# Two weight sums of each group of seven made by accumulating transfers, and the first feed-forward's first product without such a group

## The chip, the core and the metric

The kernel runs on one core of a Trainium2 chip. The metric is the device time of the whole program in microseconds (us); lower is better. The engines that matter here are TensorE (PE in the profile, with PEld for its weight loads), VectorE (DVE), ScalarE (ACT), GpSimd (POOL) and SyncE (SP), which issues nearly all DMAs.

## What is computed

The reference is a trunk of two layers on 256 rows of width 1024. Each layer is a feed-forward, a token mixer (a convolution module in layer 0, latent attention in layer 1), and a second feed-forward; a last norm follows. So there are four feed-forwards:

```python
D_MODEL, SEQ, DEPTH, D_FF = 1024, 256, 2, 2816

def swiglu_ffn(h, w1, w3, w2):
    return (jax.nn.silu(h @ w1) * (h @ w3)) @ w2

for i in range(DEPTH):
    h = h + 0.5 * swiglu_ffn(rmsnorm(h, ffn_norm1[i]), ffn1_w1[i], ffn1_w3[i], ffn1_w2[i])
    m = rmsnorm(h, mix_norm[i])
    h = h + (conv_module(m, ...) if i % 2 == 0 else mla(m, positions, ...))
    h = h + 0.5 * swiglu_ffn(rmsnorm(h, ffn_norm2[i]), ffn2_w1[i], ffn2_w3[i], ffn2_w2[i])
return rmsnorm(h, final_norm)
```

All numbers are float32.

## The kernel before

**Products.** Every float32 operand is split into a high part (`hi`, type fp32r) and a low part (`lo`, what is left), and a product is made of three matmuls (`mm3`, L330: L332 high row by low weight, L335 high by high, L336 low row by high weight). One such matmul has a 128x128 stationary block of rows and a moving weight of 128x512. The 256 rows are two blocks of 128 (`tb`).

**Weights.** They stream in blocks of 1 MB (128 x 2048 floats, eight KB to a partition), in the order of the list `blocks` (L122 to L148). `load` (L218) fetches a block through SP's queue into one of four `raw` buffers (`RAW_BUFS`), ScalarE casts its two halves to `hi` (L246), and VectorE subtracts `lo = raw - hi` (L247). There are five pairs of `hi` and `lo` (`W_BUFS`), so at most four blocks are cast ahead of the one in use. A pair comes free when TensorE is done with its block; a raw buffer when its last reader is done.

**Feed-forwards.** In each, the up product (w1 and w3) goes in six chunks of columns (loop at L876), the last one half as wide; a chunk is four blocks of weights, each used by 24 matmuls. SiLU, the product of both halves and a turn through memory (`turn`, L838, with `turn_blocks`, L465) make the gates `Gh` and `Gl`, the rows of the down product (w2), which is the class `Rows` (L745).

**Groups of seven.** One chunk of the up product (the fourth, `c == 3`, by `SEVEN_UP`) and the first four blocks of the down product (`SEVEN_DOWN`) are made, in each of the four feed-forwards, as a two by two block product with seven block products instead of eight. The two row blocks by two halves of the inner dimension are on one side, four weight blocks (W11, W12, W21, W22) on the other. `seven_products` (L366) makes the seven, each of 12 matmuls on one combination of weights and one of rows; combinations of its results are copied and added between them (L383, L386, L388, L395). The combinations of rows are made once by `whole_rows` (L347; L349), `sums_of_rows` (L338; L344) and `forms_of` (L352; L361 and L362 split them).

The combinations of weights are made by `load_seven` (L189), called for j = 0 to 6 in the place of seven blocks. It fetches the four blocks by `fetched` (L182, its DMA is L184) at j = 0 (two), 1 and 2, and sums in place, with whole-tile subtractions on VectorE by its helper `sub` (L200): at j = 1 `b11 = W12 - W11` and `b12 = W12 - W22`; at j = 2 `b11 = W22 - b11`; at j = 6 `b11 = W21 - b11`. The product j uses `b11, b11, b11, b21, b12, b22, b11`, each cast by ScalarE in halves (L214) and subtracted by VectorE (`sub` again, so also L200).

**Order.** A planner puts the instructions of each engine in order when the program is built; what is marked `urgent` (L252) goes ahead. Each engine then runs its own list in that order, and an instruction that waits holds up what stands behind it. `order` (L154) adds an order by hand; `behind` (L158) keeps a cast behind the last urgent instructions of its engine. GpSimd has little to do outside the convolution: the norms' small scalars (L429 to L432).

Of the kernel before, what the change touches and what calls it, by code (L numbers as in the profile page):

```python
# [16 lines left out]
ALU = mybir.AluOpType  # L17
# [28 lines left out]

SEVEN_UP = {0: (3,), 1: (3,), 2: (3,), 3: (3,)}
SEVEN_DOWN = (0, 1, 2, 3)  # L50

CONV_DVE = (0, 2, 4)
# [37 lines left out]
def trunk(ctx: ExitStack, tc: tile.TileContext, x, xt, first, pos, invf, gfin, wdw,  # L90
          f1w13, f1w2, f2w13, f2w2, cw1, cw2, wa, wuq, wukv, wo, wpair, out):
    nc = tc.nc
# [12 lines left out]
    def uid(s):  # L105
        n_uid[0] += 1
        return f"{s}_{n_uid[0]}"
# [16 lines left out]
    for i in range(2):  # L124
        for w13, w2 in ((f1w13, f1w2), (f2w13, f2w2)):

            n_ffn = 2 * i + (w13 is f2w13)
            for cc_ in range(5):
                if cc_ in SEVEN_UP.get(n_ffn, ()):
                    four = [w13[i, m, 2 * cc_ + a_] for a_ in range(2) for m in range(2)]  # L130
# [23 lines left out]
    def order(ins, first):  # L154
        tc.add_manual_dep(ins.ins, first.name, mybir.DependencyInfo(
            mybir.DependencyClass.NoSync, mybir.DependencyReason.DATA), reason="order")

    def behind(ins):  # L158

        for first in ahead_of.get(ins.ins.engine, [])[-BEHIND:]:  # L160
            order(ins, first)
# [20 lines left out]
    def fetched(src):  # L182
        raw = rawp.tile([P, HB], F32, tag="raw", name=uid("raw"))
        dma = nc.sync.dma_start(raw, src)  # L184
        if turns:
            order(dma, turns[-1].ins)
        return raw

    def load_seven(j, four, b, pieces):  # L189
        hi = wp.tile([P, HB], F32R, tag="hi", name=uid("hi"))  # L190
        lo = wp.tile([P, HB], F32R, tag="lo", name=uid("lo"))
        n = len(loaded)
        if j == 0:
            b[11], b[12] = fetched(four[0]), fetched(four[1])
        elif j == 1:
            b[22] = fetched(four[3])
        elif j == 2:
            b[21] = fetched(four[2])
        def sub(out, left, right):
            ins = nc.vector.tensor_sub(out, left, right)  # L200
            behind(ins)
            return ins

        if j == 1:
            sub(b[11], b[12], b[11])
            sub(b[12], b[22], b[12])
        elif j == 2:
            sub(b[11], b[22], b[11])
        elif j == 6:
            sub(b[11], b[21], b[11])  # L210
        raw = b[(11, 11, 11, 21, 12, 22, 11)[j]]
        for i in range(pieces):
            c = slice(i * HB // pieces, (i + 1) * HB // pieces)
            casts[n, i] = nc.scalar.copy(hi[:, c], raw[:, c]), sub(lo[:, c], raw[:, c], hi[:, c].bitcast(F32))  # L214
            behind(casts[n, i][0])
        return hi, lo

    def load(src, pieces=1):  # L218
        if isinstance(src, tuple) and src[0] == "seven":
            return load_seven(*src[1:], pieces)  # L220
# [31 lines left out]
    def urgent(f):  # L252

        def g(*args, **kw):
            traced = nc.cur_bb.bb.instructions
            n = len(traced)
            with tc.high_priority():
                r = f(*args, **kw)
            last = {ins.engine: ins for ins in traced[n:]}
            for engine, ins in last.items():  # L260
                ahead_of.setdefault(engine, []).append(ins)
            return r
        return g

    def load_ahead(ahead=W_BUFS - 2):
        load_to(min(len(blocks), n_used[0] + ahead))
# [5 lines left out]
    def weights(n=1, more=True):  # L272
        out = []
        for _ in range(n):
            n_used[0] += 1
            if more:
                load_ahead()
            else:
                load_ahead(0)
            out.append(loaded[n_used[0] - 1])  # L280
        return out
# [48 lines left out]
    def mm3(o, ah, al, bh, bl, start, stop, after=(), seeded=False):  # L330

        mm = nc.tensor.matmul(o, ah, bl, start=start, stop=False, skip_group_check=seeded)  # L332
        for a in after:
            order(mm, a.ins)
        nc.tensor.matmul(o, ah, bh, start=False, stop=False, skip_group_check=seeded)  # L335
        return nc.tensor.matmul(o, al, bh, start=False, stop=stop, skip_group_check=seeded)  # L336

    def sums_of_rows(x11, x12, x21, x22):  # L338


        sums = [(0, x22, x21, x22, ALU.add), (2, x21, x11, x21, ALU.subtract), (1, x11, x22, x11, ALU.subtract),
                (3, x12, x12, x11, ALU.subtract)]
        for n, out, left, right, op in sums:
            nc.vector.tensor_tensor(out, left, right, op=op)  # L344
        return sorted(((n, out) for n, out, *_ in sums), key=lambda s: s[0])
# [20 lines left out]
    def seven_products(xh, xl, forms, banks):  # L366


        def rows(a, tb):
            k = slice(4 * a, 4 * a + 4)  # L370
            return xh[:, k, tbs(tb)], xl[:, k, tbs(tb)]

        def product(a, b, fresh):
            load_ahead(W_BUFS - 1)
            (hi, lo), = weights(1, False)
            for k in range(4):
                c = slice(k * 512, k * 512 + 512)
                mm3(b, a[0][:, k], a[1][:, k], hi[:, c], lo[:, c], fresh and k == 0, k == 3, (), True)

        n0 = n_used[0]  # L380
        c11, c21, c12, c22 = banks[0, 0], banks[1, 0], banks[0, 1], banks[1, 1]
        product(rows(0, 0), c11, True)
        urgent(nc.scalar.copy)(c21, c11)  # L383
        product(forms[0], c22, True)
        kept = tmp.tile([P, 512], F32, tag="s", name=uid("p5"))
        last = urgent(nc.scalar.copy)(kept, c22)  # L386
        product(forms[1], c21, False)
        add = urgent(nc.vector.tensor_add)(c12, c21, kept)  # L388
        order(casts[n0 + 5, 0][1], add.ins)
        for high, low in gates[-NT:]:  # L390
            order(high, last.ins)
            order(low, add.ins)
        product(rows(1, 0), c11, False)
        product(forms[2], c21, False)
        add = urgent(nc.vector.tensor_add)(c22, c21, kept)  # L395
        order(casts[n0 + 6, 0][1], add.ins)
        product(forms[3], c12, False)
        product(rows(1, 1), c21, False)
# [8 lines left out]
    def tbs(tb):  # L407
        return slice(tb * P, (tb + 1) * P)
# [336 lines left out]
    class Rows:  # L745
# [6 lines left out]
        def seven(self, forms):  # L752
            seven_products(self.zh, self.zl, forms, self.o)
# [74 lines left out]
    def ffn(X, make_next, beside=lambda: None, apart=False):  # L828
        n = n_ffns[0]
        n_ffns[0] += 1  # L830
        with tc.tile_pool(name=uid("ffn"), bufs=1) as act:
            return ffn_in(act, X, make_next, beside, apart, SEVEN_UP.get(n, ()), n in SEVEN_DOWN)

    def ffn_in(act, X, make_next, beside, apart, seven_up, seven_down):
# [41 lines left out]
        for c in range(6):  # L876
# [7 lines left out]
            if seven_up and c == min(seven_up) - (1 if X.whole else 2):  # L884
                forms = forms_of(sums_of_rows(*whole_rows(X.xh, X.xl)), Gh[:, 14:], Gl[:, 14:])
            if c in seven_up:
                for key in ((0, 0), (0, 1), (1, 1), (1, 0)):
                    u[key] = bank("A", "u")
                seven_products(X.xh, X.xl, forms, {(tb, m): b for (m, tb), b in u.items()})
                beside()  # L890
                beside()
            if both and seven_down:
                z11, z21, z12, z22 = (rows4[:, n, :] for n in range(4))
                down_sums = sums_of_rows(z11, z12, z21, z22)
                first_form = forms_of(down_sums[:1], *(act.tile([P, 2, S], F32R, tag=tag, name=uid(tag))
                                                       for tag in ("s1h", "s1l")))
# [910 lines left out]
```

## Time and profile before

| what | value |
|---|---|
| median of three runs | 907.87 us (907.69 to 908.38) |
| the profiled execution, its own time | 905.75 us |
| its span, first to last instruction | 903.8 us |
| mean granted TensorE clock | 0.995 |
| matmuls | 4209 |
| DMA | 198.94 MB, 220 GB/s on the mean |

The profile is of one execution. A line of a group names the source line, the engine, the operation, what is written from what, and a count; then busy us and mean ns of one, and after the second bar the idle time of the engine before them with what ended it. A matmul overlaps the next one, so its own length says less than the number of matmuls in a stretch. "PEclk" is the clock that TensorE was granted, 1.00 being full speed. A view of stretches gives, for each, its length, then the busy time and the count of instructions of each engine, the granted clock, the busy share of the 16 DMA engines and their GB/s. A view in order of time gives start and length in us, engine, line, operation and count, and in brackets the idle time before and what ended it. A DMA line gives the count, the KB of one and the median us from issue to landing.

### The profile page before, as it was taken

The numbers are of one execution on the slowest core, as the hardware profiler recorded it, in microseconds if no ns is written. First come the engines' busy times: TensorE is split into PE (matmuls) and PEld (weight loads), VectorE is DVE, ScalarE is ACT, GpSimd is POOL, SyncE is SP. The second block draws the span as 40 slices with busy tenths as digits, with TensorE's granted clock in tenths as the row PEclk, the third lists the DMA queues.
The fourth block names the chain that finished last, engine by engine and source line by source line (L and its number), as shares of the span: only waits on it lengthen the run. The fifth ranks groups of instructions, "written<-read, shape, count | busy, mean of one in ns | idle before, by whom it ended". The sixth has DMA issues, their size and how long they took to land.

```text
span 903.8 us, 12258 instructions
## 1 busy us (share of the span) xinstructions
PE 890.2 (98%) x4209; PEld 744.1 (82%) x4209; DVE 765.3 (85%) x1104; ACT 580.7 (64%) x1005; POOL 104.2 (12%) x227
## 2 busy tenths in 40 slices
PE   9998999999999999999999999999999999999997
PEld 7886787898998888887878888888899888888886
DVE  6899999669998988999588999994768588999963
ACT  7965849579886745766475466573767576465752
POOL 1000000049972000000010000000500010000000
PEclk9999999999999999999999999999999999999999
DMA  9883947825415873948849459396544449378551
GB/s 337 324 278 96 341 171 264 356 86 202 141 47 158 317 270 99 368 150 330 303 133 342 161 171 381 89 397 216 190 175 169 158 137 350 101 257 319 173 200 47
DMA packets 71054, 198.94 MB, mean 220 GB/s; under 512 B 12368, under 2 KB 41936, under 8 KB 51664
## 3 DMA queue, kind: packets, MB, share of 16 engines
q1 hardware_dynamic: 70560, 197.47, 61.5%
q8 instruction: 33, 0.54, 0.2%
q10 hardware_dynamic: 432, 0.69, 0.2%
q14 instruction: 29, 0.24, 0.1%
HBM read 181.87 MB, written 16.25 MB: 219 GB/s over the span
## 4 chain that ended last, share of the span: by engine, by line
PE 76%; DVE 11%; DMA 6%; issue 2%; ACT 2%; SPq 1%; DVEq 0%; ACTq 0%
PE u L332 11%; PE u L336 11%; PE u L335 11%; PE o L332 8%; PE o L335 8%; PE o L336 8%; DVE lo L200 3%; PE u L993 3%; PE gate L993 3%; DMA raw<-in_f2w 3%; DVE raw L200 2%; PE u L403 2%; PE o L1229 2%; DVE lo L247 1%; DMA hd<-rows 1%
## 5 line engine op out<-in xcount | busy, mean ns | idle before, releaser
L247 DVE TENSOR_TENSOR lo<-raw,hi 128x1024 fp32r<-128x1024 f32 (+1 forms) x228 | 266.8, 1211 | 35.0 <-ACT hi L246 33.7
L246 ACT CAST hi<-raw 128x1024 fp32r<-128x1024 f32 (+1 forms) x230 | 228.6, 1044 | 78.7 <-DMA raw<-in_f2w 30.5
L332 PE MATMUL u<-lo,Xh 128*128 128x512 f32 x592 | 231.7, 391 | 2.6 <-DVE lo L200 1.9
L335 PE MATMUL u<-hi,Xh 128*128 128x512 f32 x592 | 231.0, 390 | 0.0
L336 PE MATMUL u<-hi,Xl 128*128 128x512 f32 x592 | 230.8, 391 | 0.0
L214 ACT CAST hi<-raw 128x1024 fp32r<-128x1024 f32 x112 | 111.4, 1049 | 65.5 <-DVE raw L200 55.6
L200 DVE TENSOR_TENSOR lo<-raw,hi 128x1024 fp32r<-128x1024 f32 x112 | 132.4, 1215 | 6.6 <-ACT hi L214 6.6
L332 PEld LDWEIGHTS u<-lo,Xh 128*128 128x128 f32 x592 | 111.6, 188 | 27.9 <-DVE lo L200 3.9
L336 PEld LDWEIGHTS u<-hi,Xl 128*128 128x128 f32 x592 | 111.5, 188 | 24.3 <-DVE Xl L457 0.5
L335 PEld LDWEIGHTS u<-hi,Xh 128*128 128x128 f32 x592 | 111.5, 188 | 23.0
L336 PE MATMUL o<-hi,Gl 128*128 128x512 f32 (+1 forms) x276 | 106.6, 386 | 0.0
L335 PE MATMUL o<-hi,Gh 128*128 128x512 f32 (+1 forms) x276 | 106.5, 386 | 0.0
L332 PE MATMUL o<-lo,Gh 128*128 128x512 f32 (+1 forms) x276 | 106.2, 387 | 0.2 <-DVE lo L200 0.2
L429 POOL TENSOR_TENSOR ms<-ss 128x1 f32<-128x1 f32 x16 | 8.1, 512 | 607.2 <-ACT junk L421 607.2
L200 DVE TENSOR_TENSOR raw<-raw,raw 128x2048 f32<-128x2048 f32 x32 | 73.0, 2280 | 2.4 <-DMA raw<-in_f1w 1.1
L332 PEld LDWEIGHTS o<-lo,Gh 128*128 128x128 f32 x276 | 51.8, 188 | 11.5 <-DVE lo L200 1.0
L336 PEld LDWEIGHTS o<-hi,Gl 128*128 128x128 f32 x276 | 51.8, 188 | 10.6
L335 PEld LDWEIGHTS o<-hi,Gh 128*128 128x128 f32 x276 | 51.9, 188 | 10.2
L1082 DVE SCALAR_TENSOR_TENSOR acc<-V,dw,acc 128x128 f32<-128x128 f32 (+1 forms) x174 | 53.9, 391 | 0.0
L1103 ACT ACTIVATE prod<-V,dw 128x128 f32<-128x128 f32 (+1 forms) x128 | 45.8, 415 | 2.0 <-POOL Y L1104 1.0
L845 ACT CAST Gh<-gb 128x512 fp32r<-128x512 f32 (+1 forms) x32 | 18.0, 565 | 32.2 <-DMA gb<-gd 32.2
L789 DVE SCALAR_TENSOR_TENSOR h<-o,rh,h 128x512 f32<-128x512 f32 (+1 forms) x18 | 12.9, 719 | 29.5 <-PE o L336 29.5
(265 smaller groups left out, 1311.9 us busy)
## 6 DMA issues: line engine op xcount, KB each, us to landing
raw<-in_f2w SPq DMA_DIRECT2D x66, 1024.0 KB, 6.5
raw<-in_f1w SPq DMA_DIRECT2D x62, 1024.0 KB, 6.9
raw<-in_cw SPq DMA_DIRECT2D x12, 1024.0 KB, 5.6
gd<-gt SPq DMA_DIRECT2D x160, 64.0 KB, 3.1
gb<-gd SPq DMA_DIRECT2D x24, 256.0 KB, 2.8
rows<-gd SPq DMA_DIRECT2D x16, 256.0 KB, 3.0
raw<-in_wo SPq DMA_DIRECT2D x4, 1024.0 KB, 4.7
hd<-rows SPq DMA_DIRECT2D x56, 64.0 KB, 2.2
```

What stands on the lines that cost most here:

```text
L200: ins = nc.vector.tensor_sub(out, left, right)
L214: casts[n, i] = nc.scalar.copy(hi[:, c], raw[:, c]), sub(lo[:, c], raw[:, c], hi[:, c].bitcast(F32))
L246: casts[len(loaded), i] = (nc.scalar.copy(hi[:, c], raw[:, c]), low.tensor_sub(lo[:, c], raw[:, c], hi[:, c].bitcast(F32)))
L247: low.tensor_sub(lo[:, c], raw[:, c], hi[:, c].bitcast(F32)))
L332: mm = nc.tensor.matmul(o, ah, bl, start=start, stop=False, skip_group_check=seeded)
L335: nc.tensor.matmul(o, ah, bh, start=False, stop=False, skip_group_check=seeded)
L336: return nc.tensor.matmul(o, al, bh, start=False, stop=stop, skip_group_check=seeded)
L403: mm = nc.tensor.matmul(o, al if kind == "x" else ah, bl if kind == "l" else bh, start=start and n == 0, stop=stop and n == len(kinds) - 1)
L993: mm = nc.tensor.matmul(u[:, t], w[:, c], X.x[:, k, t], start=(k == 0), stop=(k == KT - 1))
L1082: dve_last.append(nc.vector.scalar_tensor_tensor(out if j == j1 - 1 else y, v, w, y, op0=ALU.mult, op1=ALU.add))
L1103: prods_last.append(nc.scalar.activation(p, v, AF.Copy, scale=w))
L1229: p = nc.tensor.matmul(o[tb, d], (Zl if kind == "x" else Zh)[:, f, tbs(tb)], (lo if kind == "l" else hi)[:, c], start=(f, kind) == (0, "l" ...
```

## The change

The first feed-forward (number 0) leaves `SEVEN_UP`: its fourth chunk is made like the others, with four blocks of 24 matmuls. The other seven groups stay. In them, the two sums at j = 1 are no longer made by VectorE: GpSimd issues two DMAs that read a weight block a second time and add it, on the way, to the tile in SBUF (`accum_op`). Such a transfer adds only, so the signs are turned: `b11 = W11 + W12`, `b12 = W12 + W22`; the sums at j = 2 and 6 stay on VectorE as additions, and the sums of rows and two of the additions after products change their signs to match. The new DMAs have no order by hand.

```diff
-SEVEN_UP = {0: (3,), 1: (3,), 2: (3,), 3: (3,)}
+SEVEN_UP = {1: (3,), 2: (3,), 3: (3,)}
...
-        def sub(out, left, right):
-            ins = nc.vector.tensor_sub(out, left, right)
+
+        def sub(out, left, right, op=ALU.subtract):
+            ins = nc.vector.tensor_tensor(out, left, right, op=op)
             behind(ins)
             return ins
 
         if j == 1:
-            sub(b[11], b[12], b[11])
-            sub(b[12], b[22], b[12])
+
+            nc.gpsimd.dma_start(b[11], four[1], accum_op=ALU.add)
+            nc.gpsimd.dma_start(b[12], four[3], accum_op=ALU.add)
         elif j == 2:
-            sub(b[11], b[22], b[11])
+            sub(b[11], b[22], b[11], ALU.add)
         elif j == 6:
-            sub(b[11], b[21], b[11])
+            sub(b[11], b[21], b[11], ALU.add)
...
-        sums = [(0, x22, x21, x22, ALU.add), (2, x21, x11, x21, ALU.subtract), (1, x11, x22, x11, ALU.subtract),
-                (3, x12, x12, x11, ALU.subtract)]
+        sums = [(0, x22, x21, x22, ALU.subtract), (2, x21, x11, x21, ALU.subtract), (1, x11, x22, x11, ALU.subtract),
+                (3, x12, x12, x11, ALU.add)]
...
-        add = urgent(nc.vector.tensor_add)(c12, c21, kept)
+        add = urgent(nc.vector.tensor_sub)(c12, kept, c21)
...
-        add = urgent(nc.vector.tensor_add)(c22, c21, kept)
+        add = urgent(nc.vector.tensor_sub)(c22, kept, c21)
```

## The prediction

> **What bounds the kernel now.** I read the page first: the share of each engine, and the chain that ended last.
>
> ```profile
> PE 890.2 (98%) x4209; PEld 744.1 (82%) x4209; DVE 765.3 (85%) x1104; ACT 580.7 (64%) x1005; POOL 104.2 (12%) x227
> PE 76%; DVE 11%; DMA 6%; issue 2%; ACT 2%; SPq 1%; DVEq 0%; ACTq 0%
> ```
>
> TensorE is busy nearly the whole span, and the chain runs through it. So a change is worth what it does to the number of matmuls, and to the few places where they do not follow each other at full pace. A busy PE is modelled, so I count matmuls per stretch instead: the views of stretches, first around the group that the change drops (first feed-forward, fourth chunk), then inside it.
>
> ```profile
> 60.00:100.00 40.00, 34.81 (x137) 27.23 (x136) 38.63 (x39) 24.20 (x35) 0.00 (x0) 0.91 0.58 198
> 100.00:140.00 40.00, 40.00 (x178) 33.05 (x177) 37.47 (x40) 24.67 (x39) 0.00 (x0) 1.00 0.61 214
> 76.00:84.00 8.00, 5.12 (x17) 3.80 (x16) 7.03 (x9) 7.51 (x9) 0.00 (x0) 0.79 0.37 100
> 90.00:100.00 10.00, 8.05 (x28) 5.85 (x27) 10.00 (x13) 9.38 (x16) 0.00 (x0) 0.83 0.88 326
> PE u L332 <- DVE lo L200: 4.8, 2, 2.9
> ```
>
> The columns are the stretch, its length, busy us (count) of PE, PEld, DVE, ACT and POOL, the granted clock, the DMA share and GB/s. A clean 40 us holds 178 matmuls, so one takes 40 / 178 = 0.2247 us. The 40 us of this group hold 137: 41 x 0.2247 = **9.2 us are lost there**. The last row, from the waits of that same stretch, says for what: the low part of a weight (L200, a DVE subtraction in the group's loader). The wait itself is 4.8 us; the rest is the slow pace after it, with a granted clock of 0.79 and 0.83 in the two stretches with the waits. DVE is busy 38.6 of these 40 us, so it is DVE that is late.
>
> The seven groups that stay lose far less. In a clean 20 us there are 89 to 90 matmuls:
>
> ```profile
> 140.00:160.00 20.00, 19.83 (x87) 15.88 (x86) 18.61 (x19) 17.95 (x35) 0.00 (x0) 1.00 0.90 326
> 360.00:380.00 20.00, 19.90 (x88) 16.16 (x87) 20.00 (x21) 15.62 (x17) 0.00 (x0) 1.00 0.96 352
> 400.00:420.00 20.00, 19.73 (x87) 15.80 (x86) 20.00 (x23) 15.04 (x21) 0.00 (x0) 1.00 0.61 218
> 520.00:540.00 20.00, 19.90 (x88) 16.20 (x87) 17.74 (x20) 11.90 (x15) 0.00 (x0) 1.00 0.47 152
> 800.00:820.00 20.00, 19.90 (x89) 16.14 (x88) 20.00 (x21) 14.95 (x17) 0.00 (x0) 1.00 0.95 350
> 840.00:860.00 20.00, 20.00 (x89) 16.23 (x88) 20.00 (x23) 15.93 (x22) 0.00 (x0) 1.00 0.59 209
> ```
>
> Against 90 they lack 3 + 2 + 3 + 2 + 1 + 1 = 12 matmuls, 12 x 0.2247 = 2.7 us in all. That is the most that freeing DVE in them can give.
>
> **Part one: the first feed-forward's group goes.** A group is seven products of 12 matmuls, 84; the plain chunk is two halves by two row blocks by eight by three, 96. So 12 x 0.2247 = +2.7 us. DVE loses, by these rows, four sums, six low parts (three weights of two pieces), one whole-row sum, four sums of rows, four low parts of forms:
>
> ```profile
> L200 DVE TENSOR_TENSOR lo<-raw,hi 128x1024 fp32r<-128x1024 f32 x112 | 132.4, 1215 | 6.6 <-ACT hi L214 6.6
> L200 DVE TENSOR_TENSOR raw<-raw,raw 128x2048 f32<-128x2048 f32 x32 | 73.0, 2280 | 2.4 <-DMA raw<-in_f1w 1.1 <-DMA raw<-in_f2w 1.0
> L344 DVE TENSOR_TENSOR xs<-xs 128x512 f32<-128x512 f32 x16 | 10.9, 682 | 0.0
> L362 DVE TENSOR_TENSOR Gl<-xs,Gh 128x512 fp32r<-128x512 f32 x16 | 10.8, 684 | 0.0
> L349 DVE TENSOR_TENSOR xs<-Xh,Xl 128x2048 f32<-128x2048 f32 x4 | 9.1, 2285 | 0.0
> ```
>
> 4 x 2.28 + 6 x 1.215 + 2.285 + 4 x 0.682 + 4 x 0.684 = 9.1 + 7.3 + 2.3 + 2.7 + 2.7 = 24.1 us less on an engine that was behind by 9. What is late next? The four weights are still fetched, now by the plain loader, with 24 matmuls (5.4 us) to each instead of 12, and the DMA runs at 198 GB/s in that stretch, while one MB in 5.4 us asks for about 195; after it 0.99 of the DMAs was a catching up that is now spread. The two products of SiLU that were urgent are so no longer; 24 us of free DVE hide that. I take all of the 9.2 us back: **-9.2 + 2.7 = -6.5 us**. Bounds: nothing back, +2.7; all back, -6.5.
>
> **Part two: in seven groups two DVE sums become two accumulating transfers.** Per group DVE loses 2 x 2.28 = 4.6 us. SP's queue is not touched; POOL gets the two issues. Both signs of a sum have one price (L344 holds both). No row shows an accumulating transfer, so the question is by when it must have landed. Take the down group of the second feed-forward, from the order of time (start, length):
>
> ```profile
> 381.21 2.36 DVE L200 TENSOR_TENSOR lo<-raw,hi 128x1024 fp32r<-128x1024 f32 x2 [0.78 <-ACT hi L214]
> 384.56 2.29 DVE L200 TENSOR_TENSOR raw<-raw,raw 128x2048 f32<-128x2048 f32 x1 [0.99 <-DMA raw<-in_f2w]
> 386.97 2.00 ACT L214 CAST hi<-raw 128x1024 fp32r<-128x1024 f32 x2 [1.24 <-DVE raw L200]
> 401.56 0.39 PE L332 MATMUL o<-lo,s1h 128*128 128x512 f32 x1
> 404.28 0.40 PE L332 MATMUL o<-lo,rows 128*128 128x512 f32 x1
> ```
>
> The first row is the first product's low parts: they end at 383.57, and only then may the first matrix be added to in place. The second row is the sum that goes. The fourth is the second product's first matmul, which needs that sum cast; the fifth the third product's, which needs a further sum on top. After the landing: cast 1.05 and low part 1.2, ready 2.3 us later, so the second product allows 401.56 - 383.57 - 2.3 = 15.7 us. For the third, both pieces must be cast and their low parts taken (2.00 + 1.2, about 3.4 with the handovers), then the sum 2.28 and a cast and low part 2.3: 8.0 us, so 404.28 - 383.57 - 8.0 = **12.7 us from the last low part to the landing**. The same for the up group:
>
> ```profile
> 326.56 2.31 DVE L200 TENSOR_TENSOR lo<-raw,hi 128x1024 fp32r<-128x1024 f32 x2
> 349.48 0.39 PE L332 MATMUL u<-lo,Gh 128*128 128x512 f32 x1
> ```
>
> The third product starts 12 x 0.2247 = 2.7 us after the second, at 352.2: 352.2 - 328.87 - 8.0 = **15.3 us**. The second matrix's sum is wanted only for the fifth product, 8 us later still, so it may land second.
>
> The price by the nearest rows: one MB alone, one MB among the group's own fetches (first the down group's, then the up group's), the rate in the latter stretch, and a small POOL instruction:
>
> ```profile
> raw<-in_wo SPq DMA_DIRECT2D x4, 1024.0 KB, 4.7
> raw<-in_f2w SPq DMA_DIRECT2D x4, 1024.0 KB, 8.0
> raw<-in_f2w SPq DMA_DIRECT2D x4, 1024.0 KB, 7.4
> DMA packets 1253, 4.94 MB, mean 411 GB/s; under 512 B 142, under 2 KB 654, under 8 KB 692
> L432 POOL TENSOR_TENSOR R<-ms,neghalf 128x1 f32<-128x1 f32 x12 | 6.8, 565 | 1.0
> ```
>
> It must read a MB of SBUF besides the MB of weights. Low end: like a lone plain one, 4.7. High end: like two crowded ones in a row and an issue on POOL, 2 x 8.0 + 0.6 = 16.6 (down), 2 x 7.4 + 0.6 = 15.4 (up). I take one crowded landing, one more MB at 411 GB/s (2.5 us), and an issue: 8.0 + 2.5 + 0.6 = 11.1 (down), 10.5 (up), because the group's own fetches are still on the way when it starts, and nothing is behind them:
>
> ```profile
> 384.00:391.00 7.00, 7.00 (x33) 5.79 (x32) 6.43 (x6) 3.14 (x4) 0.00 (x0) 1.00 0.76 306
> 391.00:404.00 13.00, 13.00 (x59) 10.78 (x58) 12.97 (x15) 7.71 (x12) 0.00 (x0) 1.00 0.37 95
> ```
>
> That is under 12.7 and 15.3: hidden by the weights that are cast ahead. (The Trainium skill, Collectives: The Full Stack, section on the bandwidth ceiling, says that an adding transfer moves half the bytes of a copy in the same time, because it reads two sources; the bare transport of one MB at 411 GB/s would become 5.1 us by that. No run yet shows it; it would put the landing inside both limits too.)
>
> Queues behind the new waits: POOL is idle in all these rows (0.00), so its two issues hold up nothing until the next norm. ACT's cast of the sum waits for the landing; behind it stand casts of gates and forms, on DVE the low part and behind it the gates' products and turns. They bear the same limit, as long as the planned order puts them ahead of the cast. What it gives: at most the 2.7 us; but these lie at the sixth and seventh products, whose own sum and casts crowd DVE at the end of the group, 15 us after the sums that go. I take **0**, keeping 0 to -2.7.
>
> **The sum.** Against the profiled execution, 905.75 us (span 903.8): 905.75 - 6.5 = 899.25. The median of the runs shown, 907.87, lies 2.12 above it, so **901.4 us**.
>
> **Rivals.**
> *The transfers land too late (slower).* At the high end, 16.6 and 15.4, the third product is late by 3.9 us in each of four down groups and 0.1 in each of three up groups: 15.9 us, 917.3. It decides from 12.7 us on: at 14.3 (four times 1.6) part one is eaten up, and from 14.8 the kernel is slower by over 0.2%. For it: the second transfer shares the DMAs with the first, or may be issued ahead of it. Against: the DMAs at 0.37 from 391 on. Chance 0.26.
> *POOL is slow to issue beside a busy DVE.* DVE runs without a break from 384 to 404 (6.43 of 7, 12.97 of 13). If an issue had to wait for an unbroken run of one DVE group, 4.6 us such as the two sums together, the landing comes to 15.7 and 15.1: 4 x 3.0 = 12 us, 913.4. Chance 0.04. (The Trainium skill, SBUF — State Buffer, section Who interferes with whom, is where this comes from: a transfer issued by GpSimd starves while VectorE holds the shared port pair, though it excepts the two-input operation that fills DVE here. That exception is why the chance is small.)
> *The first feed-forward stays late.* If half of the 9.2 us comes back elsewhere before 140 us, because the plain chunk's weights now arrive no earlier (0.99 DMA share after 100), then 907.87 + 2.7 - 4.6 = 906.0. DVE's 24 us speak against. Chance 0.13. That the dropped group had no real cost would be this case's far end, 910.6.
>
> **How the numbers follow.** Forecast 0.57 (its own range 898 to 904, the 2.7 us either way); the rivals 0.26, 0.04, 0.13. From 898 to 918 holds nearly all of the forecast and of the third rival, and half of the first two: about 0.83. A measurement can tell 0.2%, 1.8 us: faster (below 906.05) is the forecast plus half of the third rival, 0.63; same, the rest of it and the onset of the first, 0.08; slower 0.29.
>
> **What would show it.** Between 60 and 100 us about 178 matmuls, granted clock 1.00, and no wait for L200: part one right. TensorE's 4209 matmuls becoming 4221. The landing of the accumulating transfer in each group below 12.7 us after the first product's low parts: part two right; above it, waits of PE for L200 in every down group at its third product, and the clock below 1.00 there, prove the first rival. An issue on POOL of several us proves the second. DVE's busy time should fall by 24 + 7 x 4.6 = 56 us, to about 709; if the time falls no more than part one says, DVE was no bound in the seven groups.

## The result, and the profile after

The changed kernel takes **954.69 us** (median, 952.96 to 960.98), the kernel before in the same comparison 907.78 (905.99 to 908.38): a ratio of **1.053, 95% interval 1.048 to 1.058**. It is slower, 53 us above the forecast and outside the range. The profiled execution took 954.62 us, its span is 952.8, the mean granted clock 0.983. Of the runs below, one of experiment 5, the profiled one (945.1 us), counts as slow: that experiment's ratio is of its other three (924.57 to 930.79 us), and what is read in its trace is of that run.

First the page of the kernel after: the engines, the chain that ended last, the queue of GpSimd's own DMAs (packets, MB, share of 16 engines over the span), the gates' casts on ScalarE, and the issues of eight of the fourteen accumulating transfers.

```profile
PE 904.2 (95%) x4221; PEld 752.4 (79%) x4221; DVE 711.4 (75%) x1069; ACT 571.6 (60%) x993; POOL 118.0 (12%) x241
q0 software_dynamic: 2016, 14.68, 7.6%
PE 61%; DMA 18%; DVE 13%; issue 3%; ACT 3%; SPq 1%; POOL 0%; DVEq 0%; ACTq 0%; POOLq 0%
L847 ACT CAST Gh<-gb 128x512 fp32r<-128x512 f32 (+1 forms) x32 | 17.9, 565 | 56.6 <-DMA gb<-gd 56.6
raw<-in_f2w POOLq DMA_DIRECT2D x8, 1024.0 KB, 12.9
```

The counts came out as forecast: 4221 matmuls, and DVE busy 711.4 us (forecast about 709). But the chain has moved: DMA's share went from 6% to 18%, PE's from 76% to 61%. ScalarE stood 56.6 us before the casts of gates for a small transfer, `gb<-gd`, the way back of a turn; in the kernel before that was 32.2, with part one of the change alone (experiment 1) 39.7.

Next the stretches of the kernel after. The columns are those of the prediction. The first is the first feed-forward, then come all the 20 us rows of the seven groups that lack at least 6 matmuls, and last the 13 us that the prediction showed of the down group of the second feed-forward.

```profile
60.00:100.00 40.00, 40.00 (x178) 33.12 (x177) 28.05 (x33) 21.57 (x32) 1.09 (x1) 1.00 0.82 286
120.00:140.00 20.00, 14.59 (x57) 11.38 (x56) 15.49 (x19) 14.86 (x36) 0.00 (x0) 0.90 0.22 56
140.00:160.00 20.00, 20.00 (x83) 16.38 (x82) 17.72 (x18) 14.95 (x22) 0.00 (x0) 0.93 0.81 310
340.00:360.00 20.00, 17.32 (x76) 13.69 (x75) 13.24 (x15) 10.45 (x13) 0.00 (x0) 1.00 0.41 98
360.00:380.00 20.00, 16.84 (x71) 12.64 (x70) 20.00 (x21) 12.24 (x15) 0.00 (x0) 1.00 0.77 274
400.00:420.00 20.00, 14.43 (x63) 11.28 (x61) 8.36 (x11) 7.64 (x13) 0.00 (x0) 0.98 0.69 162
420.00:440.00 20.00, 17.30 (x67) 13.85 (x68) 20.00 (x21) 15.44 (x18) 0.00 (x0) 0.85 0.61 215
540.00:560.00 20.00, 16.50 (x70) 12.70 (x70) 20.00 (x23) 11.02 (x14) 0.00 (x0) 1.00 0.27 82
560.00:580.00 20.00, 19.23 (x84) 15.08 (x83) 19.68 (x21) 15.72 (x18) 0.00 (x0) 1.00 0.96 357
600.00:620.00 20.00, 14.96 (x59) 11.93 (x58) 19.59 (x22) 14.54 (x22) 0.00 (x0) 0.83 0.46 135
820.00:840.00 20.00, 15.83 (x62) 12.29 (x61) 20.00 (x23) 11.93 (x17) 0.00 (x0) 0.91 0.30 89
840.00:860.00 20.00, 18.64 (x80) 14.58 (x79) 19.42 (x21) 14.81 (x16) 0.00 (x0) 1.00 0.99 363
880.00:900.00 20.00, 13.24 (x47) 10.10 (x46) 17.66 (x20) 14.31 (x20) 0.00 (x0) 0.83 0.30 74
391.00:404.00 13.00, 13.00 (x59) 10.74 (x59) 4.80 (x7) 0.62 (x1) 1.76 (x2) 1.00 0.99 292
```

The first feed-forward is clean: 178 matmuls at clock 1.00 where 137 stood. The loss is in the groups that stayed. Against 90 matmuls in 20 us the twelve rows lack 33 + 7 + 14 + 19 + 27 + 23 + 20 + 6 + 31 + 28 + 10 + 43 = 261, that is 261 x 0.2247 = 58.6 us. Less the 9.2 and the 2.7 us that were lost before, plus 12 more matmuls (2.7), this makes 49.4; the span is 49.0 longer. So, by this count, the whole difference lies in the seven groups.

The last row tells how it begins. TensorE still has its 59 matmuls, from weights cast ahead. But the DMA share is 0.99 where it was 0.37, and ScalarE has done one cast in 13 us. What runs on the DMAs in that group, by the view of DMA (queues with packets, MB and share; then issues with the median us to landing), first after, then the like stretch of before:

```profile
q0 software_dynamic: 288, 2.10, 53.9%
q1 hardware_dynamic: 1552, 2.67, 41.2%
raw<-in_f2w POOLq DMA_DIRECT2D x2, 1024.0 KB, 15.0
gb<-gd SPq DMA_DIRECT2D x1, 256.0 KB, 15.3
gd<-gt SPq DMA_DIRECT2D x8, 64.0 KB, 13.1
```

```profile
gd<-gt SPq DMA_DIRECT2D x8, 64.0 KB, 1.8
gb<-gd SPq DMA_DIRECT2D x2, 256.0 KB, 2.6
```

The two sums take more than half of all 16 engines for 19 us. The turns of the last gates, issued through SP's queue, share the engines with them: 64 KB that landed in 1.8 us now take 13.1, and the way back 15.3 instead of 2.6. The order of time of the same stretch shows which engines stand still for it (start, length; in brackets the idle time before and what ended it):

```profile
393.94 0.88 POOL L208 DMA_DIRECT2D raw<-in_f2w  x1 [61.39 <-DMA raw<-in_f2w]
394.25 0.33 SPq L481 DMA_DIRECT2D gb<-gd  x1
394.58 1.12 POOL L207 DMA_DIRECT2D raw<-in_f2w  x1
397.57 12.26 SPq L476 DMA_DIRECT2D gd<-gt  x8
409.53 0.62 ACT L847 CAST Gh<-gb 128x512 fp32r<-128x512 f32 x1 [14.06 <-DMA gb<-gd]
410.19 0.69 DVE L847 TENSOR_TENSOR Gl<-gb,Gh 128x512 fp32r<-128x512 f32 x1 [10.92 <-ACT Gh L847]
411.96 1.99 ACT L216 CAST hi<-raw 128x1024 fp32r<-128x1024 f32 x2 [1.43 <-DMA raw<-in_f2w]
416.51 2.29 DVE L201 TENSOR_TENSOR raw<-raw,raw 128x2048 f32<-128x2048 f32 x1
417.33 0.58 ACT L260 COPY o<-o 128x512 f32<-128x512 f32 x1
```

`gb<-gd` is issued at 394.25, between the two sums, and ScalarE's cast of it starts at 409.53, after 14.06 us in which ScalarE did nothing. DVE stands behind it for 10.92. In ScalarE's list the cast of the sum (411.96) and the copy of a product's result (417.33; L260 lies in the helper `urgent`) come behind this cast of gates. The sum itself lands only 17.3 us after its issue at 394.58, that is at 411.9, so here its own landing came last; the copy is late behind both. TensorE's waits over the whole span (us in total, times, longest), by what they wait for:

```profile
PE o L334 <- DVE lo L201: 15.0, 5, 5.1
...
PE o L334 <- DVE Gl L847: 5.0, 1, 5.0
...
PE o L334 <- ACT o L260: 4.1, 1, 4.1
```

There is no single one: low parts, gates and copies (and, between these rows, sums of results, 5.1 and 4.6 us) are late in turn, whatever stood next in the two lists.

### The profile page after: what moved, and what is told of

The parts are those of the page before. It is cut to its first block, busy times and chain, and to the rows that moved or that the text cites. A ratio compares the mean times of both kernels' runs of the same rounds, so it can differ in the third digit from the quotient of the medians.

```text
span 952.8 us, 12303 instructions
## 1 busy us (share of the span) xinstructions
PE 904.2 (95%) x4221; PEld 752.4 (79%) x4221; DVE 711.4 (75%) x1069; ACT 571.6 (60%) x993; POOL 118.0 (12%) x241
## 3 DMA queue, kind: packets, MB, share of 16 engines
q0 software_dynamic: 2016, 14.68, 7.6%
## 4 chain that ended last, share of the span: by engine, by line
PE 61%; DMA 18%; DVE 13%; issue 3%; ACT 3%; SPq 1%; POOL 0%; DVEq 0%; ACTq 0%; POOLq 0%
DMA raw<-in_f2w 8%; PE o L334 8%; PE o L337 8%; PE o L338 8%; PE u L334 7%; PE u L337 7%; PE u L338 7%; DMA gd<-gt 5%; DVE lo L201 4%; PE u L995 3%; PE gate L995 3%; PE u L405 2%; DVE lo L249 2%; DVE raw L201 1%; ACT hi L216 1%
## 5 line engine op out<-in xcount | busy, mean ns | idle before, releaser
L249 DVE TENSOR_TENSOR lo<-raw,hi 128x1024 fp32r<-128x1024 f32 (+1 forms) x236 | 275.8, 1213 | 46.2 <-ACT hi L248 45.3
L248 ACT CAST hi<-raw 128x1024 fp32r<-128x1024 f32 (+1 forms) x238 | 236.5, 1044 | 96.0 <-DMA raw<-in_f2w 32.0
L334 PE MATMUL u<-lo,Xh 128*128 128x512 f32 x612 | 239.1, 391 | 2.6 <-DVE lo L201 2.6
L337 PE MATMUL u<-hi,Xh 128*128 128x512 f32 x612 | 238.4, 390 | 0.0
L338 PE MATMUL u<-hi,Xl 128*128 128x512 f32 x612 | 238.3, 390 | 0.0
L201 DVE TENSOR_TENSOR lo<-raw,hi 128x1024 fp32r<-128x1024 f32 x98 | 115.2, 1218 | 53.0 <-ACT hi L216 52.9
L216 ACT CAST hi<-raw 128x1024 fp32r<-128x1024 f32 x98 | 97.0, 1046 | 70.7 <-DVE raw L201 31.6
L334 PEld LDWEIGHTS u<-lo,Xh 128*128 128x128 f32 x612 | 114.9, 188 | 28.1 <-DVE lo L201 3.9
L338 PEld LDWEIGHTS u<-hi,Xl 128*128 128x128 f32 x612 | 114.9, 188 | 24.5 <-DVE Xl L459 0.4
L334 PE MATMUL o<-lo,Gh 128*128 128x512 f32 (+1 forms) x276 | 107.1, 388 | 0.3 <-DVE lo L201 0.3
L334 PEld LDWEIGHTS o<-lo,Gh 128*128 128x128 f32 x276 | 52.1, 189 | 11.3 <-DVE lo L201 0.7
L338 PEld LDWEIGHTS o<-hi,Gl 128*128 128x128 f32 x276 | 52.0, 188 | 10.5
L337 PEld LDWEIGHTS o<-hi,Gh 128*128 128x128 f32 x276 | 52.0, 188 | 10.4
L847 ACT CAST Gh<-gb 128x512 fp32r<-128x512 f32 (+1 forms) x32 | 17.9, 565 | 56.6 <-DMA gb<-gd 56.6
L950 ACT ACTIVATE s<-u,R 128x512 f32<-128x512 f32 (+1 forms) x48 | 30.8, 646 | 34.5 <-PE u L338 33.2
L847 DVE TENSOR_TENSOR Gl<-gb,Gh 128x512 fp32r<-128x512 f32 (+1 forms) x32 | 19.2, 620 | 30.0 <-ACT Gh L847 30.0
## 6 DMA issues: line engine op xcount, KB each, us to landing
raw<-in_f1w POOLq DMA_DIRECT2D x6, 1024.0 KB, 10.9
```

The lines of the kernel that those rows point to most:

```text
L201: ins = nc.vector.tensor_tensor(out, left, right, op=op)
L248: casts[len(loaded), i] = (nc.scalar.copy(hi[:, c], raw[:, c]), low.tensor_sub(lo[:, c], raw[:, c], hi[:, c].bitcast(F32)))
L249: low.tensor_sub(lo[:, c], raw[:, c], hi[:, c].bitcast(F32)))
L847: gates.append((nc.scalar.copy(gh, bv), nc.vector.tensor_sub(low, bv, gh.bitcast(F32))))
L950: nc.scalar.activation(s[:, :w], u[0, tb][:, :w], AF.Silu, scale=X.r[tb])
```

## The experiments

The theories. **A, landing:** the sums land too late for their products, because GpSimd issues the second matrix's transfer ahead of the first's (it does so in six of the seven groups); this is the prediction's first rival with its clause. **B, turns by large packets:** small packets of the gates' turns alternate with large, slow adding packets. **C, share:** the transfers take time of the DMA engines from everything, and how much they take decides. **D, lists:** it is ScalarE's order, gates ahead of copies, that carries the lateness to TensorE. Unless another base is named, an edit is against the changed kernel, and ratios are to the kernel before.

### 1. Part one alone

```diff
-            nc.gpsimd.dma_start(b[11], four[1], accum_op=ALU.add)
-            nc.gpsimd.dma_start(b[12], four[3], accum_op=ALU.add)
+            sub(b[11], b[12], b[11], ALU.add)
+            sub(b[12], b[22], b[12], ALU.add)
```

> Part one alone: the first feed-forward without its group, all sums of the other seven groups on VectorE as plain additions. Both theories say the same here: the stretch 60 to 100 us lost 9.2 us and the plain chunk costs 2.7 us more, so about 901.4 us, 0.7% faster than before. If it comes out at 908 or more, the loss of the change does not lie in the accumulating transfers alone.

Measured: **901.98 us** (900.03 to 903.91), ratio 0.9935 [0.9917, 0.9953]. The stretch of the first feed-forward:

```profile
60.00:100.00 40.00, 40.00 (x178) 33.13 (x177) 28.05 (x33) 21.71 (x32) 0.00 (x0) 1.00 0.82 289
```

Part one gives 5.9 us, and 901.98 is close to the forecast for the whole change. All the slowing, 954.7 - 902.0 = 52.7 us, is part two's. This is the fastest version here, and it beats both kernels.

### 2. The first matrix's transfer first

```diff
-            nc.gpsimd.dma_start(b[11], four[1], accum_op=ALU.add)
-            nc.gpsimd.dma_start(b[12], four[3], accum_op=ALU.add)
+            first = nc.gpsimd.dma_start(b[11], four[1], accum_op=ALU.add)
+            order(nc.gpsimd.dma_start(b[12], four[3], accum_op=ALU.add), first.ins)
```

> The whole change, but GpSimd issues the first matrix's transfer ahead of the second's. Theory A (the sum lands late because the other transfer goes first): its landing falls from 13 to 17 us to about 10 or 11 in every group, the loss of some 8 us a group to about 2, and the time to about 915 to 925 us. Theory B (the transfers crowd out the small packets of the gates' turns through memory, whoever goes first): the turns still land only after the two transfers, and the time stays above 940 us.

Measured: 949.71 us (948.58 to 951.74), ratio 1.046 [1.044, 1.0481]. In the seven groups the first matrix's transfer now lands 8.1, 9.8, 10.7, 9.3, 10.4, 9.2 and 10.9 us after its issue; in the changed kernel it took 9.4 to 17.3. In the order of time, in the waits of ScalarE and of TensorE:

```profile
389.72 0.87 POOL L207 DMA_DIRECT2D raw<-in_f2w  x1 [58.09 <-DVE lo L201]
390.26 1.23 POOL L208 DMA_DIRECT2D raw<-in_f2w  x1
```

```profile
ACT Gh L847 <- DMA gb<-gd: 85.2, 15, 14.0
```

```profile
PE o L334 <- ACT o L260: 17.9, 4, 6.4
```

The issue follows the low part that it waits for, and counted from that low part's end, as the prediction counts, the landings come after 8.4 to 11.3 us, within its limits of 12.7 and 15.3. Yet only 5 us come back, where A expected 30 or more. **A falls** as the main cause. What grew is ScalarE's wait for turns, 85.2 us, and TensorE's for the copy that stands behind it.

### 3 and 4. One transfer of the two

```diff
-            nc.gpsimd.dma_start(b[11], four[1], accum_op=ALU.add)
+            sub(b[11], b[12], b[11], ALU.add)
             nc.gpsimd.dma_start(b[12], four[3], accum_op=ALU.add)
```

> Part one, with only the second matrix's sum (wanted by the fifth product) by an accumulating transfer, and the first on VectorE. Theory A: nothing waits for it, about 899 to 903 us. Theory B: half of the crowding stays, so the turns are late by about half as much, 910 to 930 us.

```diff
             nc.gpsimd.dma_start(b[11], four[1], accum_op=ALU.add)
-            nc.gpsimd.dma_start(b[12], four[3], accum_op=ALU.add)
+            sub(b[12], b[22], b[12], ALU.add)
```

> Part one, with only the first matrix's sum (wanted by the second product) by an accumulating transfer, the second on VectorE. By theory A, which the issue order already spoke against, its landing of about 8 us is inside the limits of 12.7 and 15.3 and the time is 901 to 904 us. By theory B it crowds the turns as the second matrix's did (911 us) and the first product's successor waits besides: 911 to 930 us.

Measured: only the second matrix 911.32 us (910.04 to 914.82), ratio 1.0043 [1.0027, 1.0059]; only the first 931.33 (927.61 to 933.95), ratio 1.025 [1.0206, 1.0294]. Both have seven adding transfers, so the same bytes and nearly the same engine time, but the first kernel costs 9.3 us over part one alone and the second 29.4. In the down group of the second feed-forward the transfer is issued at 384.42 in the first kernel and lands 8.5 us later, in the second at 385.19 and 10.8. The waits of TensorE, first of the kernel with the second matrix's transfer, then of that with the first's:

```profile
PE o L334 <- DVE lo L201: 1.3, 4, 0.4
```

```profile
PE o L334 <- DVE lo L201: 9.9, 8, 3.7
```

Engine time alone (C) does not give that. The first matrix's sum is cast for the second product, the second's only for the fifth. A landing inside the limit still holds up ScalarE's list while its cast waits, and TensorE waits 9.9 us for low parts. (The planner orders the lists anew for each kernel, so a part of the difference may be that.)

### 5. The transfers with nobody waiting for their sums

Base: part one alone. Nothing of the computation is left out; two additions per group into memory that nobody reads are extra. They start when the first product's low parts are done.

```diff
+    spare = [dram.tile([P, HB + 64], F32, name=f"spare{i}")[:, :HB] for i in range(2)]
...
+            mark = nc.gpsimd.tensor_copy(small.tile([P, 1], F32, tag="mark", name=uid("mark")),
+                                         b["lo"][:, HB - 1:].bitcast(F32))
+            for dst, src in zip(spare, (four[1], four[3])):
+                order(nc.gpsimd.dma_start(dst, src, accum_op=ALU.add), mark.ins)
```

> Part one with all sums on VectorE, and beside them two accumulating transfers per group of the same size that start when the first product's low parts are done and that add weights to a scratch tile in device memory which nobody reads; so no product waits for them. Theory A: about 901 to 905 us. Theory B: the turns land late as in the change, and the time is above 920 us. The scratch lies in device memory and not in SBUF, so a packet may take another time than the 0.63 us seen; its length is to be read first.

Measured: 930.67 us (924.57 to 945.1), ratio 1.0226 [1.0194, 1.0258]: 28.7 us over part one alone by the medians, 26 by the ratios, though no engine waits for them. The planner orders the lists anew with them; what that costs is inside the 10.5 us of experiment 7, which has the same lists. So of part two's 52.7 us, some 26 to 29 come with the presence of the transfers, 949.7 - 930.7 = 19.0 more (21 by the ratios) when products wait for them, and 954.7 - 949.7 = 5.0 from their order. The split is rough: each kernel has lists of its own, and in experiment 11 an order alone is worth 10.2 us. It also holds only so far as adding into memory costs the engines what adding into SBUF does; an adding packet took 0.628 us at the median in both.

### 6. The real transfers in small packets

Base: the first matrix first.

```diff
-            first = nc.gpsimd.dma_start(b[11], four[1], accum_op=ALU.add)
-            order(nc.gpsimd.dma_start(b[12], four[3], accum_op=ALU.add), first.ins)
+            first = None
+            for to, src in ((b[11], four[1]), (b[12], four[3])):
+                for i in range(4):
+                    c = slice(i * 512, i * 512 + 512)
+                    dma = nc.gpsimd.dma_start(to[:, c], src[:, c], accum_op=ALU.add)
+                    if first is not None:
+                        order(dma, first.ins)
+                    first = dma
```

> The first matrix first, and each accumulating transfer cut into four of 512 columns, so that a packet is 2 KB and not 8 KB; the bytes are the same, the issues four times as many (some 0.9 us of GpSimd each). Theory B (each DMA engine takes one packet of a transfer and one of a turn in alternation, so that a 0.03 us packet of a turn waits for a 0.63 us one): the packets take about 0.16 us, the turns beside them land in about 5 instead of 12 us, and the time falls from 950 to 910 to 925 us. Theory C (the transfers take a share of the engines' time, whatever their packets): the turns and the time stay, 940 to 955 us.

Measured: 940.1 us (938.73 to 942.01), ratio 1.0351 [1.0312, 1.0391]. Between 389 and 416 us, by the view of DMA:

```profile
raw<-in_f2w POOLq DMA_DIRECT2D x8, 256.0 KB, 6.4
gb<-gd SPq DMA_DIRECT2D x3, 256.0 KB, 5.8
gd<-gt SPq DMA_DIRECT2D x8, 64.0 KB, 5.9
```

The turns land in 5.9 us instead of 11.2, as B has it, and 9.6 us come back, not more. The 2 KB packets took 0.178 us at the median, four of them 0.71, so the engines are as full for longer. And from the fourth of a group's eight on, each transfer is issued 0.25 to 0.31 us after the landing of the one three before it (in all 70 cases of this kernel and that of experiment 8; the trace shows no instruction that it waits for). So no more than three are under way at a time, and the eight last 16 to 23 us, where the two large ones took 13 to 16.

### 7. Plain copies in the place of additions

Base: 5. The lists of all five engines are the same in both.

```diff
-                order(nc.gpsimd.dma_start(dst, src, accum_op=ALU.add), mark.ins)
+                order(nc.gpsimd.dma_start(dst, src), mark.ins)
```

> As the run with two accumulating transfers beside the sums on VectorE (930.7 us), but the two transfers copy into the scratch instead of adding. Theory B: their packets take about 0.31 us, half as long, so the turns wait about half: 910 to 918 us. If adding itself does the harm, 901 to 905 us; if any second queue does it, whatever its packets, 925 us or more.

Measured: **912.45 us** (908.49 to 916.53), ratio 1.0048 [1.0025, 1.0071]. The copies cost 10.5 us over part one alone, the additions 28.7: **adding instead of copying costs 18.2 us** by the medians, in one and the same program. The queue of these transfers:

```profile
q0 software_dynamic: 2016, 14.68, 4.5%
```

For the same packets and bytes 4.5% of a span of 910.8 us against 7.6% of 952.8 in the changed kernel: 41 us of all engines against 72, by transfer 2.9 against 5.2. At the median an 8 KB packet took 0.309 us as a copy and 0.628 as an addition. By the ratios the difference is 16 us, give or take 4.

### 8. The unread additions in small packets

Base: 5.

```diff
-                order(nc.gpsimd.dma_start(dst, src, accum_op=ALU.add), mark.ins)
+                for i in range(4):
+                    c = slice(i * 512, i * 512 + 512)
+                    order(nc.gpsimd.dma_start(dst[:, c], src[:, c], accum_op=ALU.add), mark.ins)
```

> As the run with two accumulating transfers beside the sums on VectorE (930.7 us), but cut into four of 512 columns each, no product waiting for them. Theory B: 903 to 912 us. Theory C: 925 to 935 us.

Measured: 933.6 us (931.66 to 935.91), ratio 1.0279 [1.0239, 1.0319]: no gain, where B expected 903 to 912. So **B falls** in its narrow form, by which the packet's size alone decides. But the test changes more than the size: while the transfers run, a `gd<-gt` lands in 5.3 us at the median instead of 8.2, yet they last 19 to 25 us in a group instead of 13 to 17, and 57 of these small transfers are issued meanwhile instead of 29. The table behind experiment 13 shows what that does: the up groups lose less than in 5, the down groups more. That the engines are full while turns are due remains. TensorE's largest wait:

```profile
PE o L343 <- ACT o L269: 17.1, 4, 5.7
```

This copy of a result stands in ScalarE's list right behind a cast of gates, which leads to the next test.

### 9, 10 and 11. The casts of gates behind the copy

The order by hand after the fifth product takes two chunks of gates behind that copy instead of one: in 5 (kernel 9), in 2 (kernel 10), and in part one alone as a control (kernel 11).

```diff
-        for high, low in gates[-NT:]:
+        for high, low in gates[-2 * NT:]:
             order(high, last.ins)
             order(low, add.ins)
```

> As the run with two accumulating transfers that nobody waits for (930.7 us), but the casts of one more chunk of gates stand behind the copies between the seven products on ScalarE, instead of ahead of them. Theory D (the late turns reach TensorE because ScalarE stands at a gate's cast with that copy queued behind it): the wait of the third product of the down groups for the copy goes, 905 to 915 us. Theory E (the transfers harm by taking the DMA engines from everything, the list makes no difference): 925 us or more.

> The whole change with the first matrix's transfer first (949.7 us), and the same gates' casts behind the copies. Theory D: it gains what the run without any waiting product gains, some 20 us, and ends at 925 to 935 us, what is left being the wait for the sums. Theory E: 945 us or more.

> Control: part one alone (902.0 us) with the same gates' casts behind the copies and no accumulating transfer. The turns land early there, so no difference beyond 1 us either way by both theories; it is also the candidate for the fastest version.

Measured: 932.25 us (928.44 to 935.32), ratio 1.0272 [1.0229, 1.0316]; 942.74 (936.12 to 947.24), ratio 1.0384 [1.0329, 1.0439]; the control 912.16 (910.84 to 914.15), ratio 1.0049 [1.0033, 1.0065]. The waits of TensorE in kernel 9, and VectorE in its order of time:

```profile
PE o L341 <- DVE s L959: 9.5, 2, 5.4
PE o L341 <- ACT o L267: 0.6, 1, 0.6
```

```profile
401.73 0.69 DVE L854 TENSOR_TENSOR Gl<-gb,Gh 128x512 fp32r<-128x512 f32 x1 [8.00 <-ACT Gh L854]
```

The wait for the copy is gone (0.6 us), as D has it, and the time has not moved: now VectorE's list stands 8.00 us before a low part of gates, and TensorE waits for a product of SiLU behind it. The new order costs 10.2 us by itself (the control, where at most 1 us was expected); over its control the unread additions cost 20.1 us instead of 28.7, the real ones 30.6 instead of 47.7. **D holds for who carries the wait, not for the cause:** one list passes the late turn on, or the other does.

### 12 and 13. The unread transfers behind the turns

Left open by then: all transfers had been in the stretch of the turns. Base: 5; in the four down groups they start only after the seventh product's low parts. Kernel 13 is the same with plain copies, with the same lists.

```diff
+        if j == 6 and not b["up"]:
+            added(lo, four)
```

Here `added` is the mark and the two transfers of 5, which in the up groups stay where they were.

> The kernel with part one alone and two adding transfers per group that nobody reads (930.67 us), with one change: in the four down groups they start only when the seventh product's low parts are done, some 25 us later, when the turns of the last gates are over; the three up groups are as they were. The engine time that the additions take is the same (14 x 5.0 us of all 16 engines). In the kernel with the same transfers in small packets the matmuls lost lay in the down groups, about 32 of 44 us, and next to nothing in the up groups. Theory turns (what costs is that the small packets of the gates' turns come late behind the large adding ones, and the lists of ScalarE and VectorE stand with them): the loss of the down groups goes, 902 to 910 us, the turns gd<-gt of the down groups land in 2 to 4 us again, and TensorE waits in the down groups neither for ScalarE's copy nor for a sum. Theory share (10 us of all engines per group are taken from the weights, wherever they lie): 925 to 932 us, with the loss now in the plain blocks of the down product, TensorE waiting there for low parts whose casts wait for the weights' DMAs.

> The same with plain copies instead of adding transfers; every engine's list is the same as in the kernel with the later adding transfers, so this is what the changed lists and half of the engine time cost. Theory turns: 901 to 908 us, and the later adding transfers cost at most 5 us more than these. Theory share: 908 to 914 us, and the adding ones some 18 us more, as with the transfers at the early place (930.67 against 912.45).

Measured: adding 925.36 us (921.28 to 930.47), ratio 1.0195 [1.017, 1.022]; copying 913.51 (911.47 to 920.63), ratio 1.0075 [1.0047, 1.0104]. So neither theory's numbers fit throughout, and the gain of the later place, 5 us by the medians, is not clear of the noise: the intervals of 5 and 12 overlap. What moved shows in the traces. First the down group of the second feed-forward in kernel 5, then kernel 12: that group, the 20 us behind it, and an up group:

```profile
380.00:420.00 40.00, 36.95 (x151) 29.87 (x150) 33.59 (x35) 21.44 (x29) 1.85 (x3) 0.91 0.78 242
380.00:420.00 40.00, 39.63 (x172) 31.75 (x171) 38.50 (x41) 22.85 (x32) 2.71 (x3) 1.00 0.57 203
420.00:440.00 20.00, 20.00 (x87) 16.11 (x86) 8.82 (x8) 7.80 (x8) 0.00 (x0) 1.00 1.03 319
800.00:840.00 40.00, 33.69 (x137) 26.28 (x136) 32.70 (x37) 22.33 (x27) 0.00 (x0) 0.96 0.66 223
```

and ScalarE's order of time in an up group, first one of kernel 5, then the one above of kernel 12:

```profile
527.09 0.62 ACT L854 CAST Gh<-rows 128x512 fp32r<-128x512 f32 x1 [7.46 <-DMA rows<-gd]
804.77 1.14 ACT L862 CAST Gh<-rows 128x512 fp32r<-128x512 f32 x2 [6.81 <-DMA rows<-gd]
```

The down group is whole again: 172 matmuls at clock 1.00, where kernel 5 has 151 at 0.91 and part one alone 173, and `gd<-gt` lands there in 2.2 us. The transfers then run over plain blocks of the down product, at a DMA share of 1.03, and TensorE still makes 87 matmuls in 20 us.

All these kernels have 4221 matmuls, so the start of the n-th one can be set against that of the n-th with part one alone. The us lost by place, each from one execution (the whole includes up to 1.3 us elsewhere):

| kernel | four down groups | three up groups | plain blocks behind the down groups | ends of two down products | whole |
|---|---|---|---|---|---|
| changed | 31.8 | 20.8 | 0.0 | -0.4 | 53.0 |
| 2 | 30.1 | 17.1 | 0.0 | -0.4 | 46.9 |
| 5, adding (the run of 945.1 us) | 19.9 | 19.5 | 3.3 | -0.1 | 43.5 |
| 7, copying | 1.8 | 4.3 | 3.5 | -0.1 | 10.9 |
| 8, adding in small packets | 26.0 | 4.1 | 3.3 | -0.1 | 34.3 |
| 12, adding, later | -0.4 | 16.3 | 3.6 | 8.6 | 28.9 |
| 13, copying, later | -0.1 | 2.3 | 3.6 | 3.6 | 10.4 |

Kernel 5's row is of an execution 14 us over its median, so a usual one loses less, and where is not known. In the down groups the later place takes the loss from 19.9 us (26.0 in kernel 8) to nothing, so there the theory of turns (B without the packet's size) is right. The up groups, where nothing was moved, still lose 16.3; the expectation had taken them as harmless from kernel 8, though in kernel 5's trace they lose 19.5, and there too ScalarE stands for the way back of a turn, `rows<-gd`. Adding costs 11.9 us over copying in 12 and 13, and by the table most of it lies in these up groups.

The ends of two down products lose 8.6 us instead, and that far the theory of share (C) is right. In the first of the two, the weights fetched beside the additions land in 17.1 us; ScalarE stands 5.4 and 4.2 us for them, VectorE then makes eight low parts in one run of 9.8 us, and the sums into `h`, which stand behind these in its list, are late, so that TensorE waits 3.0 us for the next rows (2.0 us in one with copies). The plain blocks run at a slower pace in every kernel with unread transfers, copying ones too: 120 matmuls behind the group take 28 us instead of 27.2, at clock 1.00. Why is not shown.

## Why the prediction was wrong, point by point

- **What bounds the kernel, and part one: right.** 178 matmuls at clock 1.00 between 60 and 100 us, 4221 matmuls, DVE 711.4; alone 901.98 us, where the sum said 901.4. The third rival (first feed-forward stays late, 906.0) falls.
- **Part two, the landing: right in size, when issued first.** 11.1 and 10.5 us were forecast; 8.4 to 11.3 were measured from the same start, the end of the low part. Behind the second transfer the first lands up to 17.3 us after its issue.
- **Part two, the limits: the wrong measure.** They were taken from when TensorE needs the sum, as if only the sum's own cast, low part and product hung on it. Inside the limits the kernel still took 949.7.
- **The failed step is "Queues behind the new waits" together with "nothing is behind them".** The prediction looked for free engines' lists and for weights on the DMAs. It said that SP's queue is not touched, and judged the DMAs free by a share of 0.37 from 391 us on. That share was the turns of the last gates: few bytes (95 GB/s), but the casts in ScalarE's list, and through them both lists, hang on them. The transfers took the share to 0.99, and the turns from 1.8 us to 13.1. It also set the gates' casts behind the cast of the sum; in the built order a cast of gates stood ahead of it (409.53 before 411.96) and waited 14.06 us for the way back of its turn. That the late turns are what costs is shown for the down groups, by experiment 12; in the up groups, with 20.8 of the 53.0 us, it rests on ScalarE's waits for `rows<-gd`.
- **The price of an addition: half seen.** That an adding transfer takes the engines twice as long was weighed only for the landing. (The Trainium skill, Collectives: The Full Stack, section on the bandwidth ceiling, gives a collective's adding step half the rate of its copying step because two sources are read; the traces agree for these transfers, 0.628 us a packet against 0.309.) What it does to others was left out: 16 to 18 us by experiment 7.
- **First rival:** its clause, the second transfer ahead of the first, is true and worth 5 us; its waits for L201 in the down groups show; its price of 15.9 us was for a landing at 16.6, and the main loss lies elsewhere. **Second rival:** the issues of 1 MB on POOL took 0.81 to 1.23 us, not 4.6, and in experiment 5 twelve of the fourteen lay under a VectorE that was busy throughout (0.81 to 1.16): it falls.
- **The signs:** "landing below 12.7: part two right" was a wrong sign. Experiment 2 meets it and is 47.7 us slower than part one alone.

What stays open: how much of the 10.5 us of the copies is the planner's new order and how much their engine time (3.5 us of it is the slower pace in plain blocks, where no copy runs); why that pace is slower; what the turns alone cost in the up groups, where nothing was moved; why the order of experiment 11 costs 10.2 us by itself. Turns in larger packets, and transfers moved in the up groups, were not tried.

## What to carry to other kernels

A low DMA share does not say that the DMAs are free: look which transfers make it up, who waits for them, and how late they may come. When work moves from an engine to the DMAs, count the engine time it takes there (an addition took twice a copy) and place it where no short, awaited transfer runs; then look what the weights beside it lose. A slack read from the consumer's end holds for one operand only; every instruction behind the waiting one in the same list needs its own.

## What the runs showed of the hardware

- An adding packet of 8 KB occupied a DMA engine 0.628 us (copy 0.309), one of 2 KB 0.178 (changed kernel, 7 and 6); the adding queue took 7.6% of the engines for 14.68 MB, the copying one 4.5%.
- No more than three transfers of 256 KB in 128 rows, issued one after the other by GpSimd, were under way at a time (70 of 70 cases in 6 and 8).
- Two adding transfers of 1 MB from another queue stretched 64 KB in small packets from 1.8 to 13.1 us. While such transfers ran, the median of `gd<-gt` was 11.7 us in the changed kernel, 8.2 in 5, 5.3 with small packets (8) and 4.9 with copies (7), else 2.7 to 3.7. (The Trainium skill, DMA: Bandwidth & Descriptors, section Queues, rings and completion order, says that an engine goes round its queues packet by packet; the small transfers came late here beside a second queue, but no trace here shows the order of the packets on one engine.)
- A wait of TensorE costs more than its length: the waits of L334 in the groups add up to 41 us, the loss is 58.6, and in six of the twelve rows the granted clock was 0.83 to 0.93.
